# A two-layer encoder trunk on one core: where down's first weights lie, when the last pair's stores are issued, and how the last squares are summed

## The chip, the cores and the metric

The kernel runs on one core of a Trainium2 chip. The metric is the device time of one execution in microseconds (us). Three runs of the kernel before gave 2606.36, 2611.0 and 2601.78 us: median 2606.36.

The names are those of the profile: PE is the matrix engine (TensorE), PEld its weight loads, DVE is VectorE, ACT is ScalarE, POOL is GpSimd, SP is the engine that issues nearly all DMAs, in the order of the program.

## The reference

Two layers over 1024 tokens of width 1024, all float32. The part of a layer that matters here is its end:

```python
h = rms_norm(x, g_ffn[l]) * (1 + sc_f) + sh_f
gate, up = split_cols(h @ w_gu[l], (FFN_HIDDEN, FFN_HIDDEN))       # 1024 -> 2 x 2816
x = x + gt_f * ((jax.nn.silu(gate) * up) @ w_down[l])              # 2816 -> 1024
```

Behind it follows, in the first layer, the next layer's RMSNorm and its input projection; in the second, the trunk's last RMSNorm and the output. Attention in three head groups comes ahead of it and is not touched.

## The kernel before, in words

**Matmuls.** Each float32 operand is split in two parts: a high part, which ScalarE casts (`act.copy`, a CAST in the profile), and the rest, which VectorE subtracts (a TENSOR_TENSOR). A product is three matmuls: high by high, low by high, high by low (`mm3`).

**Gate/up.** The hidden width of 2816 is 22 column groups of 128, taken as 22 passes q (gate and up in turn, two passes to a pair b, so 11 pairs). Each pass computes a 2 x 2 block product with seven products in place of eight, in the order 11, 21, t2, t1, t3, 22, t4 (`PRODUCTS`). Their activations lie in SBUF tiles h11, h21, ht2, ht1, ht4, h22, ht3 (each a high and a low part), which stay for the whole stage and are the stationary side's partner in every pass. A product accumulates in a bank of PSUM named ps_w; ScalarE copies it to a tile u, or VectorE adds it to one. When a pair is done its four blocks (tiles sg) become seven operands for down; `g_steps` gives the pair 13 steps, of which step 3 stores three operands to DRAM (gpd), steps 8 to 10 subtract (DVE) and store one, steps 11 and 12 store three. One step is taken after each product of the following passes, so a pair's stores run beside the next pair's products. After the last pair nothing follows in gate/up.

**Down.** Again seven products, `DOWN`, each of 11 k-tiles t: 77 units u = 11 i + t. A unit multiplies a tile of weights (w11, w12, w21, w22 or their sums) by an operand read back from gpd (graw, two units to a load, `b_load`), both split into tiles wpt (8 buffers, two to a unit), with 12 matmuls into four banks ps_d. `Ahead.fill(4)` keeps four units split ahead. The loop over u first issues what is due at that unit: w12 of t at unit t, w21 and w22 of t at unit 4 + 2t, `w_sums` at unit 8 + 2t, and loads of the residual x (xb from xd, `x_back`) in four groups of four. w11 of every t and two loads of graw are issued ahead of the loop (L1934 to L1937), then the last pair's remaining steps are run all at once (`g_finish(0)`, L1940), then the third load of graw (L1942).

**Where tiles lie.** The pools of one side of SBUF are a stack. h11 and h21 lie at the right end, ht3 below them, and so on. A tile that takes the place of an older one waits for the last reader of that one. In the kernel before, pool wa holds w11 (11 tiles of 2 KB a partition) below w21 in the place of ht3, h21 and h11: w11 of t = 0 and 1 lie where ht3's high part lay.

**Order.** During down SP's instructions are pinned in program order; the other engines' order is a scheduler's, made before the run, and each works in order. Each DMA also waits for the eighth DMA before it.

**End of down.** `residual` adds each bank to x. The sums of squares of the second half of the tokens come from four odd chunks, summed in one tile beside the last units, and four even chunks, each in a tile of its own; `rstd_cols` multiplies each of these five tiles by a vector of ones in PE (ps_st), four columns of 128 tokens, accumulating over the tiles. In the first layer it stands after two chunks of the next projection (`c_first`, ps_c) and its spread over partitions (ps_r) after a third; `h_chunk` then makes the normalized activations (nt, hh, hl). In the second layer it stands after seven transposes (ps_f), and the output is scaled and stored.

Of the kernel before, what the change touches and what calls it, by code (L numbers as in the profile page):

```python
# [20 lines left out]
D = 1024  # L21
S = 1024
KC = D // P
# [62 lines left out]
def trunk(ctx: ExitStack, tc, A, C, out):  # L86
# [9 lines left out]
    def open_pool(name, bufs=1, side="left", space=None):  # L96
        kw = dict(name=name, bufs=bufs, side=side, reuse_waits="tile")
        if space is not None:
            kw["space"] = space
            if space == PSUM:  # L100
                kw.pop("side")
        cm = tc.tile_pool(**kw)
        p = cm.__enter__()
        return cm, p

    def close(cm):
        cm.__exit__(None, None, None)
# [87 lines left out]
    def blocks(pl):  # L195
        return Blocks([pl.tile([P, S], F32, name="xb", tag=f"x{n}") for n in range(KC)])
# [215 lines left out]
    def rstd_cols(ssqs, width, nt, sp_, psp, tag="mm", newton=False):  # L412

        ps = psp.tile([P, 512], F32, name="ps_st", tag=tag)
        for j in range(nt):
            for i, s in enumerate(ssqs):
                pe.matmul(
                    ps[:, j : j + 1],
                    s[:, j * P : (j + 1) * P],
                    ones,  # L420
                    start=(i == 0),
                    stop=(i == len(ssqs) - 1),
                )
        r = sp_.tile([P, 8], F32, name="rstd", tag="rstd", bufs=2)
        if newton:
            inv_sqrt(r[:, :nt], ps[:, :nt], width, sp_)
            return r
        act.activation(r[:, :nt], ps[:, :nt], AF.Sqrt, bias=epst, scale=1.0 / width)
        dve.reciprocal(r[:, :nt], r[:, :nt])
        return r  # L430
# [60 lines left out]
    ps_cm, psl = open_pool("ps0", bufs=8, space=PSUM)  # L491
    x_cm, xp = open_pool("x", side="left")
    xt = xp.tile([P, KC, S], F32, name="xt")
# [198 lines left out]
    for l in range(2):  # L692
# [198 lines left out]
        norm = {0: c_norm(0, psc[0])}  # L891
# [583 lines left out]
        ps_cm, psl = open_pool("ps1", bufs=8, space=PSUM)  # L1475
# [32 lines left out]
        for ki in range(5):  # L1508
# [4 lines left out]
            if ki == 0:  # L1513
                r = rstd_cols([gss[N - 1]], norms[N - 1][1], 8, atp, psl, newton=True)
# [24 lines left out]
        x_cm, xp = open_pool("x", side="left")  # L1539
        xt = blocks(xp)  # L1540
        for n in range(KC):
            sp.dma_start(xt[:, n, :], xd[:, n, :])
        nt_cm, ntp = open_pool("nt", side="left")
# [51 lines left out]
        ssq = square_sum(ntp, xt, 0, 1)  # L1595
        for i, n in enumerate((6, 7, 0, 1, 2, 3, 4, 5)):
# [11 lines left out]
            if i == 1:  # L1608
                norm = rstd_rows(ssq, ntp, psl)
# [7 lines left out]
        ssq = square_sum(ntp, xt, 1, 1)  # L1617
# [111 lines left out]
        def g_step():  # L1729
            if steps:  # L1730
                steps[0].pop(0)()
                if not steps[0]:
                    steps.pop(0)

        def g_finish(pairs):

            while len(steps) > pairs:
                g_step()
# [115 lines left out]


        nt_cm, ntp = open_pool("nt", side="left")
        wa_cm, wap = open_pool("wa", side="right")
        wb_cm, wbp = open_pool("wb", side="left")
        W = {}

# [8 lines left out]
        def w_first(name, t, pl):  # L1869
            W[name, t] = pl.tile([P, H], F32, name=f"w{name}", tag=f"w{name}{t}")  # L1870
            sp.dma_start(parts(W[name, t], 4), w_load(name, t))
# [4 lines left out]
        def b_load(i):  # L1876

            n = min(2, NU - 2 * i)
            t = wp.tile([P, 2, H], F32, name="graw", tag="wst", bufs=2)
            sp.dma_start(t[:, :n], gpd[:, 2 * i : 2 * i + n, :])  # L1880
            for k in range(n):
                raw[2 * i + k] = t[:, k]
# [16 lines left out]
        def at_unit(u, what):  # L1899
            due.setdefault(u, []).append(what)  # L1900
# [18 lines left out]

        for t in range(NB):  # L1920
            at_unit(t, lambda t=t: w_first("12", t, wbp))
            at_unit(4 + 2 * t, lambda t=t: w_first("21", t, wap))
            at_unit(4 + 2 * t, lambda t=t: w_first("22", t, wbp))
            at_unit(8 + 2 * t, lambda t=t: w_sums(t))
            at_unit(31 + t, lambda t=t: w_sum4(t))
            at_unit(33 + t, lambda t=t: w_again(t))
        for us, n0, half in (
            ((2, 3, 6, 7), 0, 0), ((13, 15, 17, 19), 0, 1), ((26, 28, 30, 32), 1, 1),
            ((34, 36, 38, 40), 1, 0),
        ):  # L1930
            for i, u in enumerate(us):
                at_unit(u, lambda n=n0 + 2 * i, half=half: x_back(n, half))

        for t in range(NB):  # L1934
            w_first("11", t, wap)
            if t in (1, 3):
                b_load(t // 2)  # L1937
        ahead = Ahead(units())
        ahead.fill(4)
        g_finish(0)  # L1940
        xt = blocks(xp)
        b_load(2)  # L1942
        acc_a = [psl.tile([P, 512], F32, name="ps_d", tag="mm") for _ in range(4)]
        acc_b = None
# [1 line left out]
        def norm_half(ssqs, half):  # L1946

            r = rstd_cols(ssqs, D, 4, ntp, psl)
            yield
            rows = spread(r, 0, psl)  # L1950
            yield
            for m in range(KC):
                h_chunk(ntp, rows, xt, half, m, 1, 0, 0, hh, hl, m % 2)
                yield

        def square(n, half, tag, bufs):
            sq = ntp.tile([P, H], F32, name="sq", tag=tag, bufs=bufs)
            act.activation(sq, xt[:, n, half * H : (half + 1) * H], AF.Square)
            return sq

        def square_add(ssq, n, half):
            sq = square(n, half, "sq", 2)
            dve.tensor_tensor(out=ssq, in0=ssq, in1=sq, op=ALU.add)
# [28 lines left out]
        for u in range(NU):  # L1992
            i, t = divmod(u, NB)
            num, _, bank = DOWN[i]
            for what in due.get(u, ()):
                what()
            ahead.fill(4)
            if u % 2 == 0 and (u + 6) // 2 <= (NU - 1) // 2:
                b_load((u + 6) // 2)
            if t == 0 and num == 2:  # L2000
                acc_b = [psl.tile([P, 512], F32, name="ps_d", tag="mm") for _ in range(4)]
            banks = acc_a if bank == "a" else acc_b
            a, b = ahead.have.pop(0)
            for j in range(4):
                js = slice(j * P, (j + 1) * P)
                mm3(
                    banks[j], a[:, 0, js], a[:, 1, js], b[:, 0], b[:, 1],
                    num in (1, 2, 5) and t == 0, t == NB - 1, skip_group_check=True,
                )
            next(beside, None)  # L2010
            if u >= NU - 3 and not last_layer:
                if u == NU - 3:
                    wC = []
                wC.append(split_w(w_in_src(1, C_COLS, len(wC)), 2))
            if t < NB - 1:
                continue
            m, half = {
                1: (0, 0), 2: (0, 0), 6: (0, 1), 7: (1, 1), 4: (1, 0), 5: (1, 1), 3: (0, 1),
            }[num]
            for j in range(4):  # L2020
                residual(banks[j], 2 * j + m, slice(half * H, half * H + H), 40)
            if num == 4:
                close(wa_cm)
                if last_layer:
                    fn_cm, fnp = open_pool("fin", side="right")
                    gf = fnp.tile([P, D], F32, name="gf")
                    sp.dma_start(gf, bc(A["g_final"][None, :], [P, D]))
                else:
                    h_cm, hp = open_pool("h", side="right")
                    hh = hp.tile([P, KC, S], F32R, name="hh")  # L2030
                    hl = hp.tile([P, KC, S], F32R, name="hl")
                    spill(0)
                beside = chain(early_half(), odd_squares())
        for _ in beside:
            pass
        pin([sp], False)
        evens = [square(n, 1, *(("sqe", 3) if n else ("ssq", 1))) for n in range(0, KC, 2)]
        ssqs = odd + evens
        if last_layer:
            blocks_ = [(1, j, nh) for j in range(4) for nh in range(2)]  # L2040
            turned = [out_turn(*b) for b in blocks_[:7]]
            r = rstd_cols(ssqs, D, 4, ntp, psl)
            for t in turned:
                out_scale(*t, r)
            for b in blocks_[7:]:
                out_scale(*out_turn(*b), r)
            close(fn_cm)
            close(wb_cm)
            close(nt_cm)
            continue  # L2050
# [2 lines left out]
        wC.append(split_w(w_in_src(1, C_COLS, 3), 2))  # L2053
        close(wb_cm)
        pssC = [psl.tile([P, 512], F32, name="ps_c", tag="mm") for _ in range(T0)]
        norm = norm_half(ssqs, 1)
        for n in range(KC):
            c_first(n)
            if n == 1:
                next(norm)  # L2060
            if n == 2:
                for _ in norm:
                    pass
        close(nt_cm)
# [74 lines left out]
```

## Time and profile before

| what | value |
|---|---|
| median of three runs | 2606.36 us |
| the profiled execution's own time | 2610.04 us |
| its span, first to last instruction | 2608.3 us |
| granted TensorE clock, mean | 0.975 |
| gate/up's last matmul to down's first, layer 1 | 1108.06 to 1109.73 us |
| the same, layer 2 | 2361.90 to 2364.07 us |

All times within the profile count from the span's start. In the groups, a row gives the engine, the operation, what it writes and reads, and its count; in a timeline a row begins with its start and its length, and a bracket gives how long the engine was idle before it and what ended that. SPq is the time that SP takes to issue a DMA, in which the transfer itself is not counted. The page shows two records for a float32 matmul of one column (ps_st), so 20 such instructions are 40 records.

### The profile page before, as it was taken

The numbers are of one execution on the slowest core, as the hardware profiler recorded it, in microseconds if no ns is written. First come the engines' busy times: TensorE is split into PE (matmuls) and PEld (weight loads), VectorE is DVE, ScalarE is ACT, GpSimd is POOL, SyncE is SP. The second block draws the span as 40 slices with busy tenths as digits, with TensorE's granted clock in tenths as the row PEclk, the third lists the DMA queues.
The fourth block names the chain that finished last, engine by engine and source line by source line (L and its number), as shares of the span: only waits on it lengthen the run. The fifth ranks groups of instructions, "written<-read, shape, count | busy, mean of one in ns | idle before, by whom it ended". The sixth has DMA issues, their size and how long they took to land.

```text
span 2608.3 us, 34639 instructions
## 1 busy us (share of the span) xinstructions
PE 2455.3 (94%) x12071; PEld 2024.9 (78%) x12071; DVE 1836.1 (70%) x2916; ACT 1241.4 (48%) x2335; POOL 974.2 (37%) x881
## 2 busy tenths in 40 slices
PE   5899999988899999989998999998999999998998
PEld 4677899776677777878886779987877888886887
DVE  6845999987978786377657449998587455445865
ACT  5421888943433333334543128898444333333443
POOL 5641445643643444300044224465446434430001
PEclk9999999998999999999999999999999999998999
DMA  8467205165244543296432760151624233228643
GB/s 265 141 186 232 61 18 151 39 219 176 89 146 162 169 157 123 88 290 199 135 97 68 212 191 25 25 156 43 202 65 145 93 106 105 93 97 248 203 140 108
DMA packets 291166, 356.48 MB, mean 137 GB/s; under 512 B 33080, under 2 KB 207376, under 8 KB 290992
## 3 DMA queue, kind: packets, MB, share of 16 engines
q1 hardware_dynamic: 290688, 354.14, 44.1%
q8 instruction: 95, 1.56, 0.2%
q14 instruction: 79, 0.65, 0.1%
q0 software_dynamic: 304, 0.14, 0.0%
HBM read 267.31 MB, written 87.85 MB: 136 GB/s over the span
## 4 chain that ended last, share of the span: by engine, by line
PE 47%; DVE 7%; issue 4%; DMA 3%; ACT 2%; POOL 2%; SPq 1%; POOLq 0%; DVEq 0%; ACTq 0%
PE ps_w L49 19%; PE ps_d L49 12%; PE ps_o L49 3%; PE pv L49 3%; PE ps_ab L49 2%; PE T L49 2%; PE ps_v L49 2%; PE sC L49 2%; DMA wmt<-in_w_mod_dram 1%; SPq L49 1%; DVE wpt L49 1%; DVE acc L49 1%; DVE xb L49 1%; DVE sg L49 1%; DVE ws L49 1%
## 5 line engine op out<-in xcount | busy, mean ns | idle before, releaser
L49 PE MATMUL ps_d<-wpt 128*128 128x512 f32 x1848 | 432.1, 395 | 17.7 <-ACT wpt L49 17.3
L49 PEld LDWEIGHTS ps_d<-wpt 128*128 128x128 f32 x1848 | 350.1, 190 | 95.2 <-ACT wpt L49 18.4
L49 POOL TENSOR_SCALAR pr<-pr,rs 128x1024 f32<-128x1024 f32 (+4 forms) x256 | 208.1, 815 | 223.1 <-DVE rs L49 208.9
L49 POOL TENSOR_TENSOR wlo<-wst,whi 128x1024 fp32r<-128x1024 f32 x58 | 148.4, 2561 | 263.9 <-ACT whi L49 251.5
L49 PE MATMUL pv<-pt,vs 128*128 128x256 f32 x1216 | 200.7, 296 | 11.0 <-DVE y L49 4.9
L49 DVE TENSOR_TENSOR pt<-T,pt 128x512 fp32r<-128x512 f32 x304 | 199.7, 681 | 10.2 <-ACT pt L49 8.7
L49 PE MATMUL T<-identr,pr 128*128 128x128 f32 x1320 | 191.9, 274 | 5.5 <-POOL pr L49 2.6
L49 POOL TENSOR_TENSOR wpt<-ws,wpt 128x512 fp32r<-128x512 f32 x88 | 122.9, 1399 | 191.8 <-ACT wpt L49 136.1
L49 ACT CAST wpt<-w 128x512 fp32r<-128x512 f32 x154 | 95.6, 621 | 200.2 <-PE ps_d L49 184.8
L49 ACT CAST pt<-T 128x512 fp32r<-128x512 f32 x304 | 170.0, 586 | 40.3 <-PE T L49 38.4
L49 ACT COPY u<-ps_w 128x512 f32<-128x512 f32 x132 | 77.4, 586 | 219.4 <-PE ps_w L49 219.4
L49 POOL TENSOR_TENSOR sg<-sg,u 128x512 f32<-128x512 f32 x88 | 128.0, 1455 | 142.7 <-DVE u L49 70.8
L49 PEld LDWEIGHTS pv<-pt,vs 128*128 128x128 f32 x1216 | 160.6, 189 | 25.4 <-DVE y L49 12.5
L49 PEld LDWEIGHTS T<-identr,pr 128*128 128x128 f32 x1320 | 156.6, 141 | 27.5 <-POOL pr L49 4.7
L49 DVE TENSOR_TENSOR wpt<-w,wpt 128x512 fp32r<-128x512 f32 x154 | 108.0, 701 | 90.6 <-ACT wpt L49 90.6
L49 DVE SCALAR_TENSOR_TENSOR acc<-wmt,condT,acc 128x512 f32<-128x512 f32 (+1 forms) x99 | 125.1, 1273 | 46.9 <-DMA wmt<-in_w_mod_dram 46.4
L49 ACT CAST wpt<-ws 128x512 fp32r<-128x512 f32 x176 | 108.1, 622 | 70.8 <-PE ps_w L49 31.3
L49 DVE TENSOR_TENSOR wpt<-ws,wpt 128x512 fp32r<-128x512 f32 x88 | 83.5, 949 | 79.0 <-ACT wpt L49 78.9
L49 PE MATMUL ps_w<-ht3h,wpt 128*128 128x512 f32 x352 | 114.0, 406 | 15.0 <-ACT sg L49 15.0
L49 DVE TENSOR_TENSOR ws<-wr 128x512 f32<-128x512 f32 x88 | 87.4, 995 | 56.9 <-POOL wpt L49 53.4
L49 ACT CAST whi<-wst 128x1024 fp32r<-128x1024 f32 x74 | 77.2, 1049 | 104.2 <-PE ps_o L49 46.7
L49 DVE TENSOR_REDUCE rs<-sC 128x1 f32<-128x1024 f32 x96 | 116.9, 1220 | 10.2 <-PE sC L49 9.9
(258 smaller groups left out, 6279.4 us busy)
## 6 DMA issues: line engine op xcount, KB each, us to landing
wr<-in_w_gu_dram SPq DMA_DIRECT2D x92, 512.0 KB, 4.2
gpd<-sg SPq DMA_DIRECT2D x154, 256.0 KB, 4.5
graw<-gpd SPq DMA_DIRECT2D x76, 512.0 KB, 3.6
w<-in_w_down_dram SPq DMA_DIRECT2D x110, 256.0 KB, 5.3
wmt<-in_w_mod_dram SPq DMA_DIRECT2D x47, 512.0 KB, 5.2
qk<-qkd SPq DMA_DIRECT2D x44, 512.0 KB, 7.3
wmt<-in_w_mod_dram SPq DMA_DIRECT2D x66, 256.0 KB, 3.6
qkd<-qko SPq DMA_DIRECT2D x64, 256.0 KB, 3.8
```

What stands on the lines that cost most here:

```text
L49: ins = op(*args, **kwargs)
```

## The change

Three edits.

1. Pool wa becomes two, w1 (w11) at the right end and w2 (w21) below it. So w11 lies where h21's end and h11 lay, and w21 where ht3 and h21's beginning lay.
2. `g_finish(0)` is gone. The last pair's remaining twelve steps are run three to a unit, in units 0 to 3, behind what is due there and behind the unit's load of graw. The x tiles are taken over at unit 5 (they replace the pair's sg tiles), and the first group of x loads moves from units 2, 3, 6, 7 to 6, 7, 8, 9.
3. The four even chunks' squares are added to the tile of the odd ones by VectorE, through the two buffers of tag sq, and PE multiplies one tile by the ones, not five. In the first layer the statistics stand one chunk of the projection later, and the spread too. Three tiles fewer in pool nt move pool wb (w12, w22) down by 6 KB.

```diff
-        wa_cm, wap = open_pool("wa", side="right")
+        w1_cm, w1p = open_pool("w1", side="right")
+        w2_cm, w2p = open_pool("w2", side="right")
         wb_cm, wbp = open_pool("wb", side="left")
...
-            at_unit(4 + 2 * t, lambda t=t: w_first("21", t, wap))
+            at_unit(4 + 2 * t, lambda t=t: w_first("21", t, w2p))
...
-            ((2, 3, 6, 7), 0, 0), ((13, 15, 17, 19), 0, 1), ((26, 28, 30, 32), 1, 1),
+            ((6, 7, 8, 9), 0, 0), ((13, 15, 17, 19), 0, 1), ((26, 28, 30, 32), 1, 1),
...
         for t in range(NB):
-            w_first("11", t, wap)
+            w_first("11", t, w1p)
             if t in (1, 3):
                 b_load(t // 2)
         ahead = Ahead(units())
         ahead.fill(4)
-        g_finish(0)
-        xt = blocks(xp)
         b_load(2)
...
             if u % 2 == 0 and (u + 6) // 2 <= (NU - 1) // 2:
                 b_load((u + 6) // 2)
+            for _ in range(3 if steps else 0):
+                g_step()
+            if u == 5:
+                xt = blocks(xp)
...
             if num == 4:
-                close(wa_cm)
+                close(w2_cm)
+                close(w1_cm)
...
         pin([sp], False)
-        evens = [square(n, 1, *(("sqe", 3) if n else ("ssq", 1))) for n in range(0, KC, 2)]
-        ssqs = odd + evens
+        for n in range(0, KC, 2):
+            square_add(odd[0], n, 1)
...
-            r = rstd_cols(ssqs, D, 4, ntp, psl)
+            r = rstd_cols(odd, D, 4, ntp, psl)
...
-        norm = norm_half(ssqs, 1)
+        norm = norm_half(odd, 1)
         for n in range(KC):
             c_first(n)
-            if n == 1:
+            if n == 2:
                 next(norm)
-            if n == 2:
+            if n == 3:
                 for _ in norm:
                     pass
```

SP's order at the passage of the first layer (the second is alike). gpd<-sg are the last pair's stores, graw<-gpd the loads of two units each, w11, w12 down's weights, xb the residual. Before, from the last of the eleven w11:

```order
L49 DMA w11_10001<-in_w_down_dram 128x4x128
L49 DMA gpd_94<-sg_9721 128x512
L49 DMA gpd_94<-sg_9722 128x512 x2
L49 DMA gpd_94<-sg_9721 128x512 x2
L49 DMA gpd_94<-sg_9722 128x512 x2
L49 DMA graw_10046<-gpd_94 128x1024
L49 DMA w12_10052<-in_w_down_dram 128x4x128
L49 DMA graw_10054<-gpd_94 128x1024
L49 DMA w12_10068<-in_w_down_dram 128x4x128
L49 DMA w12_10088<-in_w_down_dram 128x4x128
L49 DMA xb_10038<-xd_87 128x512
```

With the change, from the same place:

```order
L49 DMA w11_10004<-in_w_down_dram 128x4x128
L49 DMA graw_10030<-gpd_94 128x1024
L49 DMA w12_10036<-in_w_down_dram 128x4x128
L49 DMA graw_10038<-gpd_94 128x1024
L49 DMA gpd_94<-sg_9721 128x512
L49 DMA gpd_94<-sg_9722 128x512 x2
L49 DMA w12_10055<-in_w_down_dram 128x4x128
L49 DMA w12_10075<-in_w_down_dram 128x4x128
L49 DMA graw_10083<-gpd_94 128x1024
L49 DMA gpd_94<-sg_9721 128x512
L49 DMA w12_10101<-in_w_down_dram 128x4x128
L49 DMA gpd_94<-sg_9721 128x512
```

The third load of graw stood behind seven stores and stands now ahead of all of them; the first three stores stand behind the fourth load, the others behind the fifth.

ScalarE's order at the same place, around the copies of gate/up's last products (u<-ps_w, in the order 11, t2, t1, t3). Before:

```order
L49 COPY u_9867<-ps_w_9854 128x512
L49 COPY u_9900<-ps_w_9854 128x512
L49 COPY u_9916<-ps_w_9903 128x512
L49 COPY u_9932<-ps_w_9854 128x512
L49 CAST wpt_10003<-w11_9977 128x512
L49 CAST wpt_10006<-graw_9981 128x512
L49 CAST wpt_10009<-w11_9979 128x512
```

With the change:

```order
L49 COPY u_9867<-ps_w_9854 128x512
L49 CAST wpt_10006<-w11_9980 128x512
L49 COPY u_9900<-ps_w_9854 128x512
L49 CAST wpt_10009<-graw_9984 128x512
L49 CAST wpt_10012<-w11_9982 128x512
L49 COPY u_9916<-ps_w_9903 128x512
L49 CAST wpt_10015<-graw_9984 128x512
L49 CAST wpt_10018<-w11_9986 128x512
L49 COPY u_9932<-ps_w_9854 128x512
```

Down's first casts stood behind the copies and stand now between them.

VectorE's order at the end of the second layer, with the change, where before the four rows sq<-sq were not there:

```order
L49 SCALAR_TENSOR_TENSOR xb_21000<-ps_d_21155,mod1_83,xb_21000 128x512
L49 TENSOR_TENSOR sq_22540<-sq_22540,sq_22609 128x512
L49 TENSOR_TENSOR sq_22540<-sq_22540,sq_22612 128x512
L49 TENSOR_TENSOR sq_22540<-sq_22540,sq_22615 128x512
L49 TENSOR_TENSOR sq_22540<-sq_22540,sq_22618 128x512
L49 RECIPROCAL rstd_22661<-rstd_22661 128x4
```

The additions stand behind the last residual and ahead of the reciprocal.

## The prediction, made before the changed kernel ran

> **What bounds the kernel now.** I read the page first, then TensorE's waits, then the timelines and chains at the places the diff touches: the passage from gate/up to down, and the end of down, in both layers.
>
> ```profile
> PE 2455.3 (94%) x12071; PEld 2024.9 (78%) x12071; DVE 1836.1 (70%) x2916; ACT 1241.4 (48%) x2335; POOL 974.2 (37%) x881
> PE ps_d L49 <- ACT wpt L49: 17.3, 5, 7.2
> SPq L49 <- PE ps_w L49: 12.0, 1, 12.0
> ```
>
> TensorE (PE) is the bound, so only its pauses, and matmuls that run slowly after them, are to be had. The second row (us in total, times, longest) is the largest group of TensorE's waits in the whole program: down's matmuls (ps_d) for ScalarE's casts (wpt). The third row, from the DMA queue's own waits between 1094 and 1140 us, says that the sync engine's queue (SP) stood 12.0 us at one DMA until a gate/up matmul had ended. TensorE at both passages, and a stretch of 48 matmuls that nothing holds up:
>
> ```profile
> 1108.06 0.39 PE L49 MATMUL ps_w<-ht4l,wpt 128*128 128x512 f32 x1
> 1109.73 11.45 PE L49 MATMUL ps_d<-wpt 128*128 128x512 f32 x48 [1.28 <-ACT wpt L49]
> 1128.36 166.61 PE L49 MATMUL ps_d<-wpt 128*128 128x512 f32 x720 [7.18 <-ACT wpt L49]
> 1321.70 11.05 PE L49 MATMUL ps_d<-wpt 128*128 128x512 f32 x48
> 2364.07 13.09 PE L49 MATMUL ps_d<-wpt 128*128 128x512 f32 x48 [1.77 <-ACT wpt L49]
> 2383.56 167.04 PE L49 MATMUL ps_d<-wpt 128*128 128x512 f32 x720 [6.40 <-ACT wpt L49]
> ```
>
> A unit is 12 matmuls. Each layer pauses before unit 0 and again after four units. The chain of waits of the first layer (start, length, what) tells why:
>
> ```profile
> 1093.81 9.07 PE ps_w L49 x39
> 1102.88 0.37 SPq L49
> ...
> 1114.52 5.33 DMA gpd<-sg
> ...
> 1122.12 0.70 DVE sg L49
> ...
> 1123.25 4.36 DMA graw<-gpd
> ```
>
> The queue waits for the matmuls, then issues eleven weight loads and the last pair's first stores; the subtractions of that pair wait until these have landed; four more stores follow; only then goes the load of units 4 and 5 (graw), at 1123.25. In the second layer it is the same.
>
> **Part 1, the passage.** TensorE's clock (the value between the busy times and the DMA share):
>
> ```profile
> 1128.00:1132.00 4.00, 3.64 (x9) 2.83 (x10) 3.66 (x6) 3.52 (x7) 0.00 (x0) 0.50 1.02 315
> 1132.00:1136.00 4.00, 4.00 (x16) 3.21 (x15) 2.00 (x4) 1.15 (x2) 0.00 (x0) 0.81 1.01 305
> 2364.00:2368.00 4.00, 3.93 (x11) 2.83 (x12) 3.40 (x6) 3.13 (x7) 0.00 (x0) 0.72 1.13 321
> 2380.00:2384.00 4.00, 0.44 (x1) 0.45 (x2) 0.47 (x1) 1.12 (x3) 0.00 (x0) 0.50 1.04 340
> 2384.00:2388.00 4.00, 4.00 (x11) 2.99 (x11) 3.84 (x7) 2.69 (x6) 0.00 (x0) 0.50 0.57 172
> 2388.00:2392.00 4.00, 4.00 (x15) 3.19 (x14) 1.29 (x2) 1.14 (x2) 0.00 (x0) 0.79 1.07 318
> ```
>
> First layer: 1.28 before unit 0; 11.45 - 11.05 = 0.40 in the first 48 matmuls; 7.18; and after it the clock, 3.64 x 0.50 + 4.00 x 0.19 = 2.58. Together 11.44 us. Second layer: 1.77; 13.09 - 11.05 = 2.04; 6.40; 0.44 x 0.50 + 4.00 x 0.50 + 4.00 x 0.21 = 3.06. Together 13.27 us. By the Trainium skill (TensorE: Matmul & The Clock Gate, section on the HAM clock gate) the clock falls only after an idle window of about 3.4 us; here a pause of 1.77 us was enough for 0.72, so the trace differs, and by the page some 1.1 us of the 2.04 would have to come from elsewhere and might stay.
>
> Does all of it go? The first weights now wait for the h21 product instead of the t3 product:
>
> ```profile
> 1094.11 0.39 PE L49 MATMUL ps_w<-h21l,wpt 128*128 128x512 f32 x1
> 1102.66 1.26 SPq L49 DMA_DIRECT2D w<-in_w_down_dram  x2
> 1103.97 0.62 SPq L49 DMA_DIRECT2D graw<-gpd  x1
> 1106.60 7.82 SPq L49 DMA_DIRECT2D w<-in_w_down_dram  x7
> 1109.06 0.62 ACT L49 CAST wpt<-graw 128x512 fp32r<-128x512 f32 x1 [2.62 <-DMA graw<-gpd]
> ```
>
> h21 ends at 1094.5, so the series starts near 1094.7 instead of 1102.66, 8.0 us sooner. Units 0 and 1 (1103.97 to 1109.06: 5.1 us to land) are there at 1101.1, before gate/up ends at 1108.45. The load of units 4 and 5 now stands right behind the weights: 1123.25 becomes about 1106.5 (the end of the series, 1114.42, less 8.0). Even with 6 us to land it is there at 1112.5; unit 4 starts at 1108.45 + 11.05 = 1119.5 (2.76 a unit). Its splits take some 1.2 us, so that pause is covered by over 5 us.
>
> Behind it stands, in SP's new order, w12 of t 0, the load of units 6 and 7, then three stores. The load of units 6 and 7 needs unit 3's split, and this a buffer that the last gate/up product holds until 1108.45: so about 1110. The three stores go until 1112 and land by 1117 (5.33 in the chain). On VectorE (DVE) the pair's first subtraction waits for that landing, and behind it queue the splits of units 5 and 6: unit 5's is done near 1117, TensorE wants it at 1122.3. The second subtractions end near 1119, unit 6's split at 1120.3 against 1125.0. The cover is about 5 us; if it went, unit 5 would be late by what the landing exceeds 10 us. Nothing of VectorE's work is added here, only moved.
>
> What is new is on ScalarE (ACT), which works in order: the first casts now stand among the copies that empty gate/up's banks. The copy of the t1 product stands behind the cast of units 0 and 1's load:
>
> ```profile
> 1100.18 0.59 ACT L49 COPY u<-ps_w 128x512 f32<-128x512 f32 x1 [2.26 <-PE ps_w L49]
> 1102.70 0.64 PE L49 MATMUL ps_w<-h22h,wpt 128*128 128x512 f32 x2
> ```
>
> Load landed 1101.1, two casts and the copy (0.52 apart, 0.59 the last) to 1102.8; the h22 product takes that bank and wanted it at 1102.70. I charge 0.5 us a layer; the bounds are 0 (landing in 4.5) and 2 (landing in 6.7).
>
> The transfers (a window of the first layer's units, issues by line, and how long the stores and graw loads took to land there):
>
> ```profile
> 1128.00:1156.00 28.00, 27.64 (x111) 22.61 (x112) 23.47 (x38) 13.36 (x24) 0.00 (x0) 0.90 1.09 322
> w<-in_w_down_dram SPq DMA_DIRECT2D x22, 256.0 KB, 6.2
> graw<-gpd SPq DMA_DIRECT2D x6, 512.0 KB, 5.1
> DMA to landing us min/median/max: 2.0/4.4/7.7
> ```
>
> From 1094.7 to the end of unit 9 (1136.1) the new order issues 27 weight loads, 7 stores and 4 loads of x at 256 KB and 8 of graw at 512 KB: 14.2 MB, 44 us at the 322 GB/s of the first row, against 41 us. The loads run some 3 us late at unit 9; each graw is issued three units (8.3 us) before its split and six before its product, so this is absorbed. The four x loads moved from units 2 to 7 to units 6 to 9 are needed by the addition after unit 10; the last may hold VectorE 0 to 2 us, which the 5 us of cover take up. The two pools cost nothing otherwise: no instruction is added for them.
>
> **Part 2, the squares.** In each layer 32 of 40 statistics matmul records (ps_st) go, four VectorE additions come. First layer:
>
> ```profile
> 1338.46 1.13 PE L49 MATMUL ps_st<-onesr,sq 128*128 128x1 f32 x6
> 1340.67 1.15 ACT L49 ACTIVATE sq<-xb 128x512 f32<-128x512 f32 x2
> 1341.35 7.51 PE L49 MATMUL ps_st<-onesr,sq 128*128 128x1 f32 x34 [1.76 <-ACT sq L49]
> 1353.27 0.45 PE ps_r L49 x4
> 1364.84 1.30 POOL hl L49
> 1366.16 0.37 SPq L49
> ```
>
> The last squares end at 1341.82, behind a weight cast as before; an addition of 0.69 (as the pair's 0.70) brings 1342.6. Meanwhile TensorE does one more chunk of projection (12 matmuls, 2.8 us, to 1341.3). Eight records at 7.51 / 34 = 0.22 bring 1344.4, square root and reciprocal hide behind the next chunk, and ps_r comes at 1347.2 instead of 1353.27: 6.1. The chain goes on from ps_r to the last hl and the loads behind it, so it is handed on. Bounds: 3.7 if that chunk runs at half clock (2.4 more), 9 if TensorE itself were all that counts (7.0 of records and what the clock lost after them). I take 5.5, near the chain's.
>
> Second layer:
>
> ```profile
> 2588.75 2.79 DVE L49 SCALAR_TENSOR_TENSOR xb<-ps_d,mod,xb 128x512 f32<-128x512 f32 x4 [6.89 <-PE ps_d L49]
> 2593.73 4.75 PE L49 MATMUL ps_st<-onesr,sq 128*128 128x1 f32 x40
> 2598.52 0.26 ACT L49 ACTIVATE rstd<-ps_st,epst 128x4 f32<-128x4 f32 x1 [6.31 <-PE ps_st L49]
> ```
>
> The additions stand behind the four of xb, from 2591.54. Squares now share two buffers, so the third waits for the first addition: squares end near 2593.5, the last addition near 2594.3. Eight records at 4.75 / 40 = 0.119 bring 2595.3 instead of 2598.5: 3.2 us, straight off the end (bounds 2.0 at half clock, 3.8 for 32 x 0.119).
>
> **Sum.** 11.44 + 13.27 - 2 x 0.5 + 5.5 + 3.2 = 32.4 us off the profiled execution's 2610.04: 2577.6. That execution stands 3.7 above the median of the three; by this offset the median would be 2574.0. I forecast 2576.
>
> **Rivals.** *The transfers become the bound* (0.15): for it, 44 us of bytes in 41; against it, the same rate between 1128 and 1156 made no pause. If the 3 us became a pause in each layer and the clock fell as after the old one, 2 x (3 + 2.8) = 12: 2588. *The first layer's statistics are not handed on* (0.08), because the loads behind hl take as long as before from a queue that other work holds: 2581.5. *The first weights don't come sooner* (0.05): the queue could stand at another of its waits, as each of its DMAs also waits in the program for the eighth before it; then 1.28 + 0.40 + 1.77 + 2.04 = 5.5 stay: also 2581.5. *Slower* (0.03): the ring of split, graw load, stores, landing, subtraction, next split on VectorE sets the pace at units 5 and 6. To eat 32 us it must pause 13 us and 3 of clock in each layer, so a landing must take about 5 + 5 + 13 = 23 us; three times the 7.7 at most seen. With 25 us: about 2612. The Trainium skill (DMA: Bandwidth & Descriptors, section on the anatomy of one DMA) says that completion can take surprisingly long when the target is HBM, which is what these stores wait for; the rows' 2.0 to 7.7 do not bear out such a size.
>
> **Numbers.** The forecast has 0.69. Its own range is 2570 to 2584: upward the lower bounds of part 2 (3.0 less), ScalarE's upper bound (3.0 more) and 2 for the runs' spread; downward the upper bounds of part 2 (4.1 more) and ScalarE's 0 (1.0). To hold 8 in 10 it reaches up to the transfers' rival: 2566 to 2589. A measurement here tells about 0.3%, 8 us, from no change. All cases but the slower one are faster by more than that: faster 0.95, within 0.02, slower 0.03.
>
> **What would show it.** After gate/up, ps_d follows ps_w with no pause over 0.5 us and none after 48 matmuls, and the clock stays 1.00 to the end of unit 10. The queue's wait for ps_w shrinks or moves ahead of 1095. A short wait of ps_w (h22) for ScalarE's copy appears. ps_st has 8 records at each end, and ps_r comes about 6 us sooner after the last ps_d. It would be wrong if ps_d paused at units 5 to 12 for wpt, with DVE or ACT waiting for DMA gpd or graw.

## The result, and the profile after

The changed kernel takes 2579.96 us (median of four runs, 2576.94 to 2582.48); the kernel before took 2604.11 beside it (2601.78 to 2611.0). The ratio is 0.9902, with a 95% interval of 0.9879 to 0.9926: faster by about 1%. Timed once more, with four runs against seven of the kernel before, it gave 2577.18 us and 0.9881 (0.9863 to 0.99). The forecast was 2576, the range 2566 to 2589. The profiled execution took 2580.05 us, with a span of 2578.3 (before: 2610.04 and 2608.3).

The page after, TensorE's totals and the group of down's matmuls:

```profile
PE 2441.3 (95%) x12007; PEld 2015.0 (78%) x12007; DVE 1844.7 (72%) x2924; ACT 1240.8 (48%) x2335; POOL 973.9 (38%) x881
...
L49 PE MATMUL ps_d<-wpt 128*128 128x512 f32 x1848 | 423.7, 390 | 1.0 <-ACT wpt L49 0.7
```

TensorE's waits after (us in total, times, longest):

```profile
PE ps_st L49 <- DVE sq L49: 4.8, 2, 4.1
...
PE ps_d L49 <- ACT wpt L49: 0.7, 1, 0.7
```

The 17.3 us in which down's matmuls waited for casts are 0.7, and 64 records of ps_st are gone. A wait of 4.8 us is new: the statistics (ps_st) wait for the additions of squares (sq). The timeline of TensorE at both passages after:

```profile
1108.49 174.92 PE L49 MATMUL ps_d<-wpt 128*128 128x512 f32 x768
...
2342.89 0.73 PE L49 MATMUL ps_w<-h22h,wpt 128*128 128x512 f32 x2 [0.56 <-ACT u L49]
2348.58 174.90 PE L49 MATMUL ps_d<-wpt 128*128 128x512 f32 x768
```

Where each layer had a piece of 48 matmuls, a pause and a piece of 720, one piece of 768 now runs through, with no idle time before it. SP's issues in the first layer after:

```profile
1094.35 1.26 SPq L49 DMA_DIRECT2D w<-in_w_down_dram  x2
...
1105.83 0.71 SPq L49 DMA_DIRECT2D graw<-gpd  x1
...
1110.07 0.33 SPq L49 DMA_DIRECT2D graw<-gpd  x1
1110.44 2.28 SPq L49 DMA_DIRECT2D gpd<-sg  x3
```

The weights start at 1094.35 (1102.66 before), the load of units 4 and 5 goes at 1105.83 (1123.25 before), the stores behind it. The queue's wait for a gate/up matmul, 12.0 us before, is now (its waits between 1080 and 1140 us):

```profile
SPq L49 <- PE ps_w L49: 3.8, 1, 3.8
```

The difference by stretch, from the starts of matmuls in each trace (us):

| stretch | before | after | difference |
|---|---|---|---|
| start to gate/up's last ps_w, first layer | 1108.06 | 1108.27 | +0.2 |
| from there to down's last ps_d | 224.30 | 212.50 | -11.8 |
| down's last ps_d to the next layer's last ps_w | 1029.55 | 1027.58 | -2.0 |
| from there to down's last ps_d, second layer | 228.46 | 214.88 | -13.6 |
| from there to the end | 17.90 | 15.05 | -2.85 |

They sum to 30.0, the difference of the spans. 25.4 of it is the passage. The third row holds what the squares of the first layer give: 2.0 where 5.5 was forecast. This row is a thousand us long, and its far part from ps_ab on, the first matmul of the next attention's inputs, runs 979 to 986 us over the kernels below; no edit lies in it. Read nearer, the gain is 2.9 us at ps_ab (43.35 from down's last matmul, 46.28 before) and 1.8 at the first matmul of sB, some 360 us on (404.4 against 406.3). Most of what lies between is TensorE's next wait behind ps_ab (pq, which waits for VectorE's qn); before and then after:

```profile
1387.89 0.85 PE L49 MATMUL pq<-identr,qn 128*128 128x128 f32 x8 [3.50 <-DVE qn L49]
```

```profile
1374.92 1.23 PE L49 MATMUL pq<-identr,qn 128*128 128x128 f32 x8 [5.05 <-DVE qn L49]
```

The place of the squares in the chain of waits after (start, length, what):

```profile
1326.67 0.64 ACT sq L49
1327.33 2.48 DVE sq L49
1329.90 2.89 DVE sq L49
1332.89 0.70 DVE sq L49
1333.68 0.70 DVE sq L49
1334.43 1.56 PE ps_st L49 x8
1336.00 5.33 PE ps_c L49 x12
1341.33 0.66 PE ps_r L49 x4
```

The first two of the four additions take 2.48 and 2.89 us, the last two 0.70. TensorE waits 4.11 us for them, and the twelve matmuls behind the statistics take 5.33 us where 2.8 is usual. GpSimd in that stretch, from the timeline after:

```profile
1326.84 2.41 POOL L49 TENSOR_TENSOR wlo<-wst,whi 128x1024 fp32r<-128x1024 f32 x1 [2.42 <-ACT whi L49]
1329.89 2.35 POOL L49 TENSOR_TENSOR wlo<-wst,whi 128x1024 fp32r<-128x1024 f32 x1 [0.64 <-ACT whi L49]
```

Its two subtractions, for the projection's third and fourth weight tile, end at 1329.25 and 1332.24. The long additions end at 1329.81 and 1332.79: 0.56 and 0.55 us after them. The clock, from the windows after (the value between the busy times and the DMA share):

```profile
1332.00:1336.00 4.00, 1.57 (x9) 1.57 (x9) 2.17 (x3) 0.63 (x1) 0.24 (x1) 0.85 0.70 200
1336.00:1340.00 4.00, 4.00 (x10) 3.13 (x11) 0.18 (x1) 0.26 (x1) 0.00 (x0) 0.50 0.01 3
```

### The profile page after: what moved, and what is told of

Its sections match the earlier page's. It is cut to its first block, busy times and chain, and to the rows that moved or that the text cites. A ratio compares the mean times of both kernels' runs of the same rounds, so it can differ in the third digit from the quotient of the medians.

```text
span 2578.3 us, 34516 instructions
## 1 busy us (share of the span) xinstructions
PE 2441.3 (95%) x12007; PEld 2015.0 (78%) x12007; DVE 1844.7 (72%) x2924; ACT 1240.8 (48%) x2335; POOL 973.9 (38%) x881
## 4 chain that ended last, share of the span: by engine, by line
PE 48%; DVE 8%; issue 4%; DMA 3%; ACT 2%; POOL 1%; SPq 0%; POOLq 0%; DVEq 0%; ACTq 0%
PE ps_w L49 19%; PE ps_d L49 13%; PE ps_o L49 3%; PE pv L49 3%; PE ps_ab L49 2%; PE T L49 2%; PE ps_v L49 2%; PE sC L49 2%; DMA wmt<-in_w_mod_dram 1%; DVE acc L49 1%; DVE wpt L49 1%; DVE ws L49 1%; DVE xb L49 1%; DVE sg L49 1%; PE sA L49 1%
## 5 line engine op out<-in xcount | busy, mean ns | idle before, releaser
L49 PE MATMUL ps_d<-wpt 128*128 128x512 f32 x1848 | 423.7, 390 | 1.0 <-ACT wpt L49 0.7
L49 PEld LDWEIGHTS pv<-pt,vs 128*128 128x128 f32 x1216 | 161.4, 190 | 25.5 <-DVE y L49 12.7
```

The costliest lines, as they stand in the source:

```text
L49: ins = op(*args, **kwargs)
```

## The experiments

Two questions: which edit carries the 30 us, and why the first layer's squares gave 2.0 and not 5.5. All durations of parts are taken between the same two matmuls of each trace, since the stretches that no edit touches differ from one execution to the next (start to gate/up's end: 1101.68 to 1113.98 us over these kernels).

### The passage alone, and the squares alone

The passage alone: edits 1 and 2, with the squares as before.

> The change without the squares (w11's place and the interleaved stores alone). My theory: the passage carries nearly all. Down takes 212.5 us in the first layer (224.3 before, 212.5 with the whole change) and 214.9 in the second (228.5 before), so about 25 us less than before in the spans. The end of the first layer's down stays at 20.9 us from the last ps_d to ps_r and the end of the second at 17.9 us to the end. Rival (the squares' part also moves the passage, through pool wb's lower place): down's times differ from the whole change's by more than 1 us.

Measured: 2580.17 us, ratio 0.9898 (0.9873 to 0.9924). Down takes 212.54 and 214.94 us from gate/up's end, as in the whole change (212.50, 214.88). From down's last matmul ps_r comes at 20.92 us (20.75 before), and the second layer's end takes 18.35 us (17.90 before). The ratios of whole executions can't tell this kernel from the whole change (0.9902 and 0.9881).

The squares alone: edit 3.

```diff
-        evens = [square(n, 1, *(("sqe", 3) if n else ("ssq", 1))) for n in range(0, KC, 2)]
-        ssqs = odd + evens
+        for n in range(0, KC, 2):
+            square_add(odd[0], n, 1)
```

> The squares' part alone. My theory after seeing the changed kernel: 2.9 us less at the end of the second layer, next to nothing (0.5 us) from the last ps_d to ps_r in the first, because the four additions overlap GpSimd's subtractions there and take 2.5 and 2.9 us where they do; about 3 to 5 us less in all. As I predicted it: 3.2 and 5.5, so 8.7 in all.

Measured: 2600.06 us, ratio 0.9976 (0.9962 to 0.999). The second layer's end is 2.84 us shorter; in the first, ps_r comes only 0.95 us sooner after down's last matmul, and ps_ab 3.7 us (42.57). Together that is 6.5 us, which fits the ratio (6.3 us, interval 2.6 to 9.9) and is more than the 3 to 5 expected; the ratio alone would allow the 8.7 of the prediction as well. TensorE's waits of this kernel show the same wait as the whole change:

```profile
PE ps_st L49 <- DVE sq L49: 4.8, 2, 4.1
```

So the passage carries nearly all of the gain, and the squares' shortfall is the edit's own: it is there without the other two.

### One edit of the passage at a time

Edit 1 alone: w11 lies where h21 ends; the last pair's steps run all at once, ahead of the loop.

```diff
-        wa_cm, wap = open_pool("wa", side="right")
+        w1_cm, w1p = open_pool("w1", side="right")
+        w2_cm, w2p = open_pool("w2", side="right")
...
```

> Only the two pools (w11 at the right end); the last pair's stores still all at once ahead of the third load of graw. My theory: the two causes overlap. The pause before unit 0 goes (1.28 and 1.77 us, and 0.40 and 2.04 in the first 48 matmuls). The series starts 8 us sooner, but the stores still wait for gate/up's last product and their own landing, so the load of units 4 and 5 comes near 1115.5 and the pause after four units shrinks from 7.2 to about 1 to 2 us, not to nothing: down 9 to 10 us shorter in the first layer, 10 to 12 in the second. Rival (independent causes): the second pause stays at 6 to 7 us, and only 1.7 and 3.8 us go.

Measured: 2584.59 us, ratio 0.9915 (0.9894 to 0.9936); down 213.52 and 216.09 us, so 10.8 and 12.4 less than before, a little more than expected. TensorE's timeline:

```profile
1107.38 11.06 PE L49 MATMUL ps_d<-wpt 128*128 128x512 f32 x48
1118.84 164.47 PE L49 MATMUL ps_d<-wpt 128*128 128x512 f32 x720 [0.41 <-ACT wpt L49]
```

and SP's:

```profile
1104.67 8.92 SPq L49 DMA_DIRECT2D gpd<-sg  x7
1113.68 0.38 SPq L49 DMA_DIRECT2D graw<-gpd  x1
```

Edit 2 alone: the steps and their stores in units 0 to 3 (the x tiles and the first loads of x move with them), w11 where it lay.

```diff
-        g_finish(0)
-        xt = blocks(xp)
         b_load(2)
...
+            for _ in range(3 if steps else 0):
+                g_step()
```

> Only the interleaved stores (and the moved loads of x); w11 and w21 lie as before. My theory: the first pause stays (1.3 and 1.8 us, with the slow clock in the second layer), the load of units 4 and 5 is issued near 1114.5 and lands by 1120, just ahead of unit 4 at 1121.2, so the second pause goes or stays under 0.5 us: 9.5 to 10 us less in each layer. Then each part alone brings most of the passage's gain, and the two together less than their sum. Rival (independent causes): the same 19 us here, and the 5.5 us of the first pauses in the other kernel, adding up to the whole.

Measured: 2589.13 us, ratio 0.9934 (0.9911 to 0.9958); down 216.30 and 218.99 us, 8.0 and 9.5 less (9.5 to 10 expected in each layer). TensorE's timeline, then SP's:

```profile
1109.38 39.32 PE L49 MATMUL ps_d<-wpt 128*128 128x512 f32 x168 [1.50 <-ACT wpt L49]
```

```profile
1102.11 1.26 SPq L49 DMA_DIRECT2D w<-in_w_down_dram  x2
...
1113.58 0.75 SPq L49 DMA_DIRECT2D graw<-gpd  x1
```

The causes don't add: 10.8 + 8.0 in the first layer, against 11.8 together. The load of units 4 and 5 goes at 1113.68 with the one edit and at 1113.58 with the other, against 1123.25 and 1105.83. The first shortens the queue's wait for a gate/up matmul (12.0 us before, 3.8 with it; 12.2 with edit 2 alone), the second takes the stores and their landing from ahead of the load; either brings the load in time for unit 4, within 0.41 us (0.59 in the second layer). Edit 1 leaves 1.0 and 1.2 us, with the short pause after unit 3. Edit 2 leaves 3.8 and 4.1: in the first layer 1.7 at unit 0 (the pause of 1.50, weights still late) and the rest in small steps over units 0 to 16, at full clock, where only one more pause of 0.24 is listed; their cause stays open.

### Why the additions are long

Theory A: VectorE's additions, with both inputs in SBUF, are held while GpSimd's subtraction runs. Theory B: the two shared buffers pass a delay back and forth between ScalarE and VectorE. Theory C: the squares start late, because ScalarE's cast of the third weight tile stands in front of them and waits for its load.

Take the cause away: the last two subtractions on VectorE, behind the additions.

```diff
+        pin([dve], not last_layer)
         for n in range(0, KC, 2):
             square_add(odd[0], n, 1)
...
-        wC.append(split_w(w_in_src(1, C_COLS, 3), 2))
+        wC.append(split_tile(st2, 2, eng=dve))
+        wC.append(split_w(w_in_src(1, C_COLS, 3), 2, eng=dve))
+        pin([dve], False)
```

(st2 is the third tile, loaded at unit 76 as before.)

> The whole change, and the subtractions of the projection's third and fourth weight tiles (wlo) made on VectorE behind the four additions, instead of on GpSimd beside them. Theory A (VectorE's additions are held while GpSimd subtracts: 2.48 and 2.89 us where 0.70 is usual): each addition takes about 0.7, TensorE's wait for sq (4.11 us) goes, the chunk behind the statistics runs at full clock (5.33 becomes 2.8), and ps_r comes 13.8 us after down's last matmul instead of 20.4; about 6.6 us off the whole, some 2573. Theory B (the two shared buffers pass the delay between ScalarE and VectorE in turns, whoever else works): wait and ps_r stay within 1 us of 4.1 and 20.4, some 2580.

Measured: 2564.84 us in one run (some 2573 expected). VectorE, then TensorE, from the timeline:

```profile
1323.72 3.08 DVE L49 TENSOR_TENSOR sq<-sq 128x512 f32<-128x512 f32 x4 [4.80 <-ACT sq L49]
1326.72 2.35 DVE L49 TENSOR_TENSOR wlo<-wst,whi 128x1024 fp32r<-128x1024 f32 x2
...
1326.86 1.05 PE L49 MATMUL ps_st<-onesr,sq 128*128 128x1 f32 x8 [0.16 <-DVE sq L49]
```

Four additions in 3.08 us, as A has it. TensorE's wait is 0.16, the clock stays 1.00, and ps_r comes 12.91 us after down's last matmul instead of 20.36. It is handed on: ps_ab comes 7.7 us sooner than after the whole change. VectorE does the two subtractions in 2.35 us, where GpSimd took 2.41 and 2.35 for one.

Give each square a buffer of its own:

```diff
-            sq = square(n, half, "sq", 2)
+            sq = square(n, half, *(("sqe", 3) if half and n in (2, 4, 6) else ("sq", 2)))
```

> The whole change, with a buffer of its own for each of the last half's four squares (three new ones and one of the shared pair), so that no square waits for an addition. Theory B (two buffers): the wait of 4.11 us falls to 2 or less and ps_r comes 16 to 18 us after down's last matmul. Theory A (GpSimd holds the additions): the squares come sooner, the first two additions still take 2.5 and 2.9 us beside GpSimd's subtractions, and ps_r stays at 19.5 to 20.4; the total within 1 us of 2580.

Measured: 2581.21 us in one run. The chain of waits:

```profile
1326.43 2.48 DVE sq L49
1329.01 2.77 DVE sq L49
1331.87 0.70 DVE sq L49
1332.66 0.70 DVE sq L49
1333.41 1.86 PE ps_st L49 x8
1335.28 5.14 PE ps_c L49 x12
```

The additions are as long as before and ps_r comes at 20.42: theory B falls.

Add the cause where it isn't: in the second layer GpSimd is idle while the squares are added. There two subtractions that nobody reads (128x1024, released by the last residual) were put on it.

```diff
+        if last_layer:
+            x6 = xt.tiles[6]
+            for _ in range(2):
+                scr = wp.tile([P, 1024], F32R, name="wlo", tag="whl", bufs=8)
+                sub(scr, x6, x6, pool)
```

> The whole change, and in the second layer, where GpSimd stands idle while the last four squares are added (four additions in 3.07 us there), two subtractions of 128x1024 on GpSimd that nobody reads, released by the last residual. It only adds work, off the chain. Theory A (VectorE's additions are held while GpSimd subtracts): the first additions take 2.4 to 2.9 us each while GpSimd works, the four together 6.5 to 7.5, ps_st and the end come 3.5 to 4.5 us later (15.05 us from down's last matmul to the end becomes 18.5 to 19.5). Theory B (buffers and order only): additions 3.1 us together, end within 0.5 of 15.05.

Measured: 2585.46 us in one run. The second layer's end without it (the whole change), then with it:

```profile
2564.32 3.07 DVE L49 TENSOR_TENSOR sq<-sq 128x512 f32<-128x512 f32 x4
2567.45 1.05 PE L49 MATMUL ps_st<-onesr,sq 128*128 128x1 f32 x8 [0.69 <-DVE sq L49]
```

```profile
2566.06 4.57 POOL L49 TENSOR_TENSOR wlo<-xb 128x1024 fp32r<-128x1024 f32 x2 [18.72 <-DVE xb L49]
...
2565.90 6.08 DVE L49 TENSOR_TENSOR sq<-sq 128x512 f32<-128x512 f32 x4
...
2572.03 1.86 PE L49 MATMUL ps_st<-onesr,sq 128*128 128x1 f32 x8 [3.70 <-DVE sq L49]
```

The additions take 6.08 us instead of 3.07 (a little under the 6.5 expected), the wait before ps_st grows from 0.69 to 3.70, ps_st itself from 1.05 to 1.86 at the lower clock (0.50 from 2572 to 2576 us), and the end comes 18.88 us after down's last matmul instead of 15.05: 3.8 us for work that nothing waits for. Theory A is shown from both sides.

The Trainium skill says the same (SBUF — State Buffer, section "Who interferes with whom"): a VectorE instruction with two inputs in SBUF contends with a GpSimd instruction that reads SBUF, and whichever comes second is blocked for the whole of the first. For the additions these rows agree: each long one ends 0.55 us after GpSimd's subtraction.

### Squares ahead of the casts

ScalarE's order is turned, so that the four squares don't stand behind a cast that waits for its load. This doesn't forbid the overlap; it moves the additions to where only GpSimd's second subtraction is left, and away from TensorE's need.

```diff
+        pin([act], not last_layer)
         for n in range(0, KC, 2):
             square_add(odd[0], n, 1)
...
-        wC.append(split_w(w_in_src(1, C_COLS, 3), 2))
+        wC.append(split_tile(st2, 2))
+        wC.append(split_w(w_in_src(1, C_COLS, 3), 2))
+        pin([act], False)
```

> The whole change, with ScalarE's four squares ahead of its casts of the third and fourth weight tiles, which waited for their loads in front of the squares (squares from 1326.67 us, though the last residual was there at 1321.95). Theories A and C (the cast that waits for its load is what makes the squares late, and GpSimd's subtraction behind it what stretches the additions): squares from about 1322, the first additions up to 2.5 us long beside the subtraction that ends at 1324.4 and the others 0.7, no wait of TensorE ahead of ps_st, ps_r 13.8 us after down's last matmul, the first ps_ab some 5 to 6.6 us sooner than after the whole change: about 2574. If what follows ps_r is bound by the loads or by TensorE's own projection work, ps_r still comes sooner, but ps_ab by less than 3 us: 2577 to 2580.

Measured: 2569.05 us, ratio to the kernel before 0.9856 (0.9832 to 0.988). From the timeline:

```profile
1315.34 4.66 DVE L49 TENSOR_TENSOR sq<-sq 128x512 f32<-128x512 f32 x4
...
1322.87 0.95 PE L49 MATMUL ps_st<-onesr,sq 128*128 128x1 f32 x8
```

The additions are again held for 1.6 us, but they end at 1320.0 and ps_st runs at 1322.87 without waiting. ps_r comes at 12.31, ps_ab 8.3 us sooner than after the whole change. Theory C is so far right that the late squares are what puts the additions beside GpSimd; with squares nearly as late (5.3 us after down's last matmul, 5.9 after the whole change) and GpSimd away (above), only the 0.16 was lost.

Then the statistics one chunk sooner again, behind the second, as before the change:

```diff
-            if n == 2:
+            if n == 1:
                 next(norm)
-            if n == 3:
+            if n == 2:
```

> As the run with the squares ahead of the casts, and the statistics one chunk of projection sooner again (behind the second chunk, as before the change). If the squares are ready by 1327, ps_st follows the second chunk without a wait and ps_r comes about 11 us after down's last matmul; where the chain from ps_r sets the pace, ps_ab gains 2.8 us more than there: about 2571. If TensorE's work sets it, nothing more than there.

Measured: 2568.65 us, 0.9862 (0.984 to 0.9883). ps_r comes another 2.05 us sooner (10.26), ps_ab not (35.79 against 35.07). The traces show why: TensorE doesn't pause between ps_r and ps_ab in either, with 108 matmuls of the projection there in 25.5 us, against 96 in 22.8. So ps_ab is set by TensorE's own work, and with the squares ahead of the casts TensorE had no wait left ahead of ps_ab. The chain from ps_r shows only behind it: the first pq, which waits for qn, comes 0.96 us sooner (44.75 against 45.71).

Last, the kernel with the squares ahead of the casts and the whole change side by side, in more rounds:

> The same kernel as the run with the squares ahead of the casts, in more rounds and beside the whole change on the same chip. From the shares of the profile (7 to 8 us sooner at ps_ab, kept to the second layer's attention) it should come out 8 to 10 us below the whole change; if the 2569.05 against 2579.96 was chance, less than 5.

> The whole change once more, in more rounds: 2577 to 2583, as the comparison for the run beside it.

Measured: 2571.32 us (2567.44 to 2576.39; 0.9853, 0.9831 to 0.9875) and 2577.18 us (2575.81 to 2579.86). The medians are 5.9 us apart, less than the 8 to 10 expected though more than the 5 that chance was said to give, and the single runs just overlap; the profiles are 7.8 apart at ps_ab (35.52 against 43.36), and the rest goes in stretches that no edit touches. Both times the median with the squares ahead of the casts is below that of the kernel before and of the whole change.

## Why the prediction was right, step by step

**The passage: right in mechanism and size.** Forecast 11.44 and 13.27 us of pauses and clock; down became 11.8 and 13.6 us shorter. Of the rest of 0.3 to 0.4 us a layer, 0.1 lies in the baseline: the prediction took 11.05 us for 48 matmuls that nothing holds up, while 768 in 174.92 us make 10.93. Its way there held too: the series of weights was put at 1094.7 (1094.35), the load of units 4 and 5 at 1106.5 (1105.83), that of units 6 and 7 at 1110 (1110.07), the end of the three stores at 1112 (1112.72). The pieces of 768 say that the cover of 5 us was enough. The slower case needed a landing of about 23 us; after the change the stores to gpd and the loads from it land in 7.1 us at most. The section of the Trainium skill that the prediction names beside it (DMA: Bandwidth & Descriptors, on the anatomy of one DMA) describes DMAs on GpSimd's path; these are issued by SP.

**ScalarE's charge: right in one layer of two.** 0.5 us a layer was charged for the copy behind the casts. In the second layer the h22 product waits 0.56 us for it (row above). In the first no such wait shows in the timeline.

**The first matmuls of the second layer.** The prediction set against its 2.04 us a rule of the Trainium skill (TensorE: Matmul & The Clock Gate, section on the HAM clock gate), by which 1.1 us of them might come from elsewhere and stay. With the pause gone nothing stayed. But that a pause of 1.77 us is enough to lower the clock, as the prediction read it, doesn't hold in general: with edit 2 alone the same pause is there, and the clock stays at 1.00.

```profile
2352.45 47.86 PE L49 MATMUL ps_d<-wpt 128*128 128x512 f32 x201 [1.81 <-ACT wpt L49]
```

```profile
2352.00:2356.00 4.00, 3.54 (x14) 2.62 (x15) 2.94 (x5) 3.06 (x7) 0.00 (x0) 1.00 1.12 330
```

What decides it, no run here shows. The expectation of that run, the slow clock with the pause, failed here.

**The transfers: rival refuted.** The clock and the transfers in the same window, before and then after:

```profile
1124.00:1152.00 28.00, 23.64 (x93) 19.30 (x94) 19.47 (x32) 11.94 (x21) 0.00 (x0) 0.83 1.07 316
```

```profile
1124.00:1152.00 28.00, 28.00 (x125) 23.21 (x124) 24.02 (x40) 11.71 (x20) 0.00 (x0) 1.00 1.08 318
```

TensorE is busy for all 28.00 us at full clock, with 318 GB/s moved. The rival of a slower ring falls with it: no split was late.

**The first layer's squares: the step that failed.** The term was 5.5 us, with 3.7 as its lower bound; 2.0 came. The prediction said "an addition of 0.69 (as the pair's 0.70) brings 1342.6". It counted one addition behind the last square at an undisturbed duration, and did not ask what GpSimd does beside it. By the prediction's own instants ps_st would have come 10.3 us after down's last matmul (1342.6 less 1332.35); it came 13.7 after (1334.43 less 1320.76). These 3.4 us and 2.5 of clock (5.33 for 2.8), less 0.2 on ps_st, are 5.7 of the 6.1 by which ps_r should have come sooner; 0.4 were left. The bound of 3.7 allowed for the clock but not for the wait that causes it. The way on from ps_r was not as forecast either. The prediction took it through the last hl and the loads behind it; but TensorE works without a pause from ps_r to ps_ab (busy for all of 1354 to 1378 us before and of 1342 to 1364 after, at clock 1.00), and needs 25.5 us there before and 23.0 after, as one chunk of the projection more now lies ahead of ps_r. So ps_ab still gained 2.9 us (43.35 against 46.28) where ps_r gained 0.4, and the wait for qn behind it took 1.5 of that back. Without the hold the term would have been too small: with the two subtractions on VectorE (above) ps_ab comes 10.6 us sooner than before and sB 9.6, above the 9 that the prediction gave for TensorE alone.

The price could have been read before. VectorE's chain and GpSimd's timeline of the kernel before:

```profile
1321.31 1.71 DVE sq L49
1323.04 0.69 DVE sq L49
```

```profile
1320.85 1.60 POOL L49 TENSOR_TENSOR hl<-nt,hh 128x512 fp32r<-128x512 f32 x1
```

The same addition takes 1.71 us beside GpSimd's subtraction and 0.69 without, and it ends 0.57 us after that subtraction (1323.02 against 1322.45). By estimate from these rows, an addition held behind a subtraction of 2.4 us, as two of them are in the stretch, takes up to 2.3 us more (2.4 and 0.57, less 0.69), so two cost up to 4.6; 3.4 were missing.

**The second layer's end: right.** Forecast 3.2, measured 2.85. The additions end 2.99 us after the last residual, against 2.76 forecast, and the eight records take 1.05 us against 0.95.

**The sum.** 32.4 forecast against 30.0 measured on the profiled executions: 3.5 too much in the first layer's squares and 0.35 in the second's, against 0.7 too little in the passage and the 1.0 charged for ScalarE, which lies ahead of the passages compared, where the first row lost 0.2. That the smaller misses offset part of the largest one is luck. The offset of 3.7 us to the median, by which 2574 was considered, was worth nothing: the new profiled execution stands at its median (2580.05 and 2579.96).

## What to carry to other kernels

Before moving work to VectorE, look at what GpSimd does in the same microseconds, and take the duration of an instruction from rows with the same neighbour, not from the median of its group. A wait that two causes share is worth almost its whole length to whichever edit comes first, so edits that each remove one of them must not be summed. Compare kernels between two fixed instructions of the trace, and near the edit: down takes 212.50 to 212.60 us in the first layer in all nine profiles of kernels with both edits of the passage, while the 980 us from ps_ab to the next gate/up's end differ by 7 and whole executions by 10.

## What the runs showed of the hardware that was not expected

An addition of 128x512 with both inputs in SBUF, 0.70 us alone, took 2.20 to 2.89 us when it began beside a running GpSimd subtraction of 128x1024 and ended 0.55 us after it. It was seen once the other way: in the run with the statistics sooner, two subtractions on GpSimd, the second begun behind an addition, took 5.22 us, against 4.75 after the whole change. From that run's timeline:

```profile
1319.92 5.22 POOL L49 TENSOR_TENSOR wlo<-wst,whi 128x1024 fp32r<-128x1024 f32 x2 [8.78 <-ACT whi L49]
```

But where two subtractions were put beside the additions of the second layer, the first, begun 0.16 us behind an addition, took 2.27 us and the other 2.34, so there nothing was held.

After a pause of 4.11 us on TensorE the granted clock was 0.85, 0.50 and 0.80 in three windows of 4 us, a cost of 2.5 us in the next twelve matmuls alone, on top of the pause; after one of 0.56 it stayed at 1.00, and after one of about 1.8 it fell to 0.72 in one kernel and stayed at 1.00 in another. And idle work isn't free: two GpSimd instructions that nobody waits for moved the end of the kernel by 3.8 us.
